# Small constants and statistics in pools of their own, and every large on-chip buffer at a multiple of 128 bytes

## The chip, the cores and the metric

The kernel runs on one core of one Trainium2 chip, as one program launched once. The metric is device time in microseconds (us) of one execution, the median of several. The engines named below are TensorE (PE, with its weight loads as PEld), VectorE (DVE), ScalarE (ACT), GpSimd (POOL) and SyncE (SP), whose queue issues the DMAs. The on-chip memory that all of them read is called SBUF here: 128 partitions, and in each partition the same byte addresses. A buffer's address is its byte address within a partition.

## The reference, cut to what matters

Two layers of a streaming encoder on 1024 tokens of width 1024, all in float32. Each layer normalises, projects, runs three families of attention heads, merges them, reads 256 memory tokens through a cross-attention, and ends with a squared-ReLU MLP of width 4096:

```python
for layer in range(2):
    h = rms_norm(x, mix_norm_g[layer])
    proj = h @ w_in[layer]
    da_q, da_k, da_v, sb_q, sb_k, sb_v, c_q, c_kv, k_r = jnp.split(proj, pts, axis=-1)
    y_a = diff_attention(...)      # 4 heads, two softmaxes each, T5 position bias
    y_b = stick_breaking(...)      # 4 heads, sigmoid gates and a reversed running product
    y_c = latent_attention(...)    # 4 heads through low-rank projections, with rope
    x = x + jnp.concatenate([y_a, y_b, y_c], axis=-1) @ w_out[layer]
    x = x + memory_attention(rms_norm(x, memx_norm_g[layer]), mem, ...)
    h = rms_norm(x, ffn_norm_g[layer])
    x = x + jnp.square(jax.nn.relu(h @ w_ff1[layer])) @ w_ff2[layer]
```

The first and third family are causal by chunks of 64 tokens, the second token by token.

## The kernel before

Tokens are cut in two halves of 512, and each half in tiles of 128. To keep float32 accuracy on TensorE's faster float32r form, every factor of a large product is split into a high and a low part, and `mm3` issues three matmuls for each product: high by high, high by low, low by high (lines 573, 574, 575). In a call `matmul(out, stationary, moving)` the first factor is loaded into the array and the second streams through it; the profile lists the moving operand first, so `s<-h,w 128x512` is a matmul whose moving operand is the 512 columns of a tile `h` and whose stationary one is a 128-column piece of `w`.

Weights arrive by DMA in 256 KB pieces as `raw`, and `wblock` splits each on ACT (line 551) and DVE (line 552) into `w`. Activations are normalised, transposed on TensorE against the identity (line 594), split, and held transposed in `h`. There is an `h` tile for each half: that of the first half lies in a pool that grows from the low end of SBUF ("left"), that of the second half in one that grows down from the top ("right"). The MLP computes 16 groups of 256 hidden columns: `ff1` streams `h` (512 columns) past pieces of `w` (lines 573 to 575), squares the result into `hid` or, in every second group of the last part, into two `t4` tiles, and `ff2` streams `w` (512 columns) past pieces of `hid` or `t4` (line 1266). `project` and `merge` mostly stream 256 columns of `w` past pieces of `h`. Attention runs once for each half (line 1007 scores, line 1042 weighted values).

Pools are laid out one after the other by the order in which they are opened. Each buffer in a pool is rounded up to 32 bytes. The left side begins at `_BASE`, 1152 bytes, which is 9 times 128; the right side ends at `_TOP`, 229344 bytes, which is 1791 times 128 and 96 more. The first pool, `const`, holds large pieces whose sizes are multiples of 128 bytes (among them `ident`, its first, at 1152 itself) and four small ones: `mhalf` (64 bytes), `zero1`, `neglam` and `gcol` (32 each with the rounding), 160 bytes together. So all pools behind `const` begin 32 bytes past a multiple of 128, and their large buffers lie there too: `w`, `raw`, `x`, `hid`, `r`, `t2`, `t4`, `cx` and the left `h`. The statistics (`ms`, `mt`, 64 bytes, six of each) lie in the pool `temps` between larger ones; they shift what is behind them by multiples of 64 bytes that add up to 128, so that some `t4` tiles stand 32 and some 160 past a multiple of 256. The right `h` and the buffers of the second half's attention lie 96 past a multiple of 128.

The order of the instructions is not that of the code. `order_engines` takes the whole program with ranks, simulates the engines with a table of costs, and fixes the order on every engine; what may go before what follows from the tiles' contents and from which pools overlap. The constants' preparation (`setup`, rank 8) is worked in beside the first projection. In `setup` two masks are loaded as `craw`, rounded on ACT to `crnd` and stored to a scratch in DRAM: one of 512 columns and one of 1024.

Of the kernel before, what the change touches and what calls it, by code (L numbers as in the profile page):

```python
# [9 lines left out]
F32 = mybir.dt.float32  # L10
F32R = mybir.dt.float32r
AF = mybir.ActivationFunctionType
# [5 lines left out]
P = 128  # L18
_BASE, _TOP = 1152, 229344
L = 2  # L20
S = 1024
# [321 lines left out]
def trunk(ctx: ExitStack, mem: Mem, tc: tile.TileContext, a: dict, out: bass.AP):  # L343
    nc = tc.nc
    HT = NT // 2
    HS = S // 2
# [8 lines left out]
    def f(ap):  # L355
        return ap.bitcast(F32)

    dma = nc.sync.dma_start
    cp = Pool("const")
    wp = Pool("wring")  # L360
    xyp = Pool("xy")
    hp = Pool("hid")
    tp = Pool("temps")
# [16 lines left out]
    def bank(cls):  # L380
        k = turn.get(cls, 0)
        turn[cls] = k + 1
        tag = cls[k % len(cls)]
        if tag[0] == "d":
            return more[1].tile([P, 1024], F32, tag=tag)[:, :512]
        return (psp if tag[0] == "s" else more[1]).tile([P, 512], F32, tag=tag)
# [10 lines left out]
    t4spare = [None]  # L397
# [13 lines left out]
        return tp.tile([P, 512], F32R, tag="cx", bufs=4)  # L411

    def stat():
        return tp.tile([P, 16], F32, tag="ms" if t4spare[0] is None else "mt", bufs=6)

    def newx(t):
        return f(xyp.tile([P, D], F32R, tag=f"x{t}"))
# [12 lines left out]
    def bcast_row(ap1d, n):  # L430
        return bass.AP(tensor=ap1d.tensor, offset=ap1d.offset, ap=[[0, P], [1, n]])

    def growload(src, n=D):
        g = cp.tile([P, D], F32, tag="grow", bufs=2)
        dma(g[:, :n], bcast_row(src[0:1], n))
        return g
# [9 lines left out]

    loadx(0, xin)
    gmix = growload(a["mix_norm_g"][0])
    mhalf = cp.tile([P, 16], F32, tag="mhalf")
    nc.vector.memset(mhalf, -0.5)  # L450
    zero1 = cp.tile([P, 1], F32, tag="zero1")
    nc.vector.memset(zero1, 0.0)
    flipR = cp.tile([P, P], F32R, tag="flip")
    before = cp.tile([P, 2, P], F32, tag="before")
    twin = cp.tile([P, 64], F32, tag="twin")
    cs = cp.tile([P, NT, 32], F32, tag="cs")
    neglam = cp.tile([P, L], F32, tag="neglam")
    lam_init = [0.8 - 0.6 * math.exp(-0.3 * l) for l in range(L)]
    gcol = cp.tile([P, L, 4], F32, tag="gcol")
    biasd = dp.tile([8, P, 2, 256], F32, tag="biasd")  # L460
    chunkd = [dp.tile([2 * HT, HS * (h + 1)], F32, tag=f"chunk{h}") for h in range(2)]

    def setup(pool):
        mraw = pool.tile([P, 2, P], F32, tag="mraw")
        dma(mraw, a["c_mask"][:2].rearrange("m p k -> p m k"))
        dma(before, a["c_mask"][2:].rearrange("m p k -> p m k"))
        dma(twin, a["c_twin"])
        nc.scalar.activation(flipR, mraw[:, 0, :], AF.Copy)

        for h in range(2):  # L470
            n = HS * (h + 1)
            craw = pool.tile([2 * HT, S], F32, tag="craw")
            dma(craw[:, :n], a[f"c_chunk{h}"])
            crnd = pool.tile([2 * HT, S], F32R, tag="crnd")
            nc.scalar.activation(crnd[:, :n], craw[:, :n], AF.Copy)
            dma(chunkd[h], f(crnd[:, :n]))

        lp = pool.tile([P, L, 4, 64], F32, tag="lp")
        dma(lp.rearrange("p l f d -> p (l f d)"), bcast_row(a["da_lambda"][0, 0, 0:1], L * 4 * 64))
        lprod = pool.tile([P, L, 2, 64], F32, tag="lprod")  # L480
        lpv = lp.rearrange("p l (u v) d -> p l u v d", v=2)
        nc.vector.tensor_tensor(lprod, lpv[:, :, :, 0, :], lpv[:, :, :, 1, :], op=ALU.mult)
        lsum = pool.tile([P, L * 2], F32, tag="lsum")
        nc.vector.tensor_reduce(lsum, lprod.rearrange("p l u d -> p (l u) d"), axis=AX.X, op=ALU.add)
        lexp = pool.tile([P, L * 2], F32, tag="lexp")
        nc.scalar.activation(lexp, lsum, AF.Exp)
        lev = lexp.rearrange("p (l u) -> p l u", u=2)
        nc.vector.tensor_tensor(neglam, lev[:, :, 1], lev[:, :, 0], op=ALU.subtract)
        for l in range(L):
            nc.vector.tensor_scalar(neglam[:, l:l + 1], neglam[:, l:l + 1], -lam_init[l], None, op0=ALU.add)  # L490

        oh = pool.tile([32, 384], F32, tag="oh")
        dma(oh, a["c_onehot"])
        rb = pool.tile([32, 2, 8], F32, tag="rb")
        dma(rb[:, 0, :], a["rel_bias"])
        far = a["rel_bias"][15, 0:1]
        dma(rb[:, 1, :], bass.AP(tensor=far.tensor, offset=far.offset, ap=[[0, 32], [1, 8]]))
        rd = pool.tile([32, 8], F32, tag="rd")
        nc.vector.tensor_tensor(rd, rb[:, 0, :], rb[:, 1, :], op=ALU.subtract)
        ps = bank(("e2",))  # L500
        nc.tensor.matmul(ps[:8, :384], rd, oh, start=True, stop=True)
        br = pool.tile([8, 384], F32, tag="br")
        nc.scalar.activation(br, ps[:8, :384], AF.Copy)
        bd = dp.tile([8, 384], F32, tag="bd")
        dma(bd, br)
        for m in range(8):
            tt = pool.tile([P, 256], F32, tag="bt", bufs=2)
            h0 = bd[m:m + 1, 0:1]
            dma(tt, bass.AP(tensor=h0.tensor, offset=h0.offset, ap=[[1, P], [1, 256]]))
            nc.vector.tensor_tensor(tt[:, 128:], tt[:, 128:], mraw[:, 1, :], op=ALU.add)  # L510
            bb = pool.tile([P, 2, 256], F32R, tag="bb", bufs=2)
            nc.scalar.activation(bb[:, 0, :], tt, AF.Copy)
            nc.vector.tensor_tensor(bb[:, 1, :], tt, f(bb[:, 0, :]), op=ALU.subtract)
            dma(biasd[m], f(bb))
# [62 lines left out]
    def rstd_of(ms, n, d):  # L577

        nc.vector.tensor_scalar(ms, ms, 1.0 / d, EPS, op0=ALU.mult, op1=ALU.add)  # L579
        rs = stat()[:, :n]  # L580
        nc.gpsimd.tensor_tensor(rs, ms, mhalf[:, :n], op=ALU.pow)  # L581
        return rs
# [20 lines left out]
    def norm_T(x_, grow, hi, lo, cls):  # L603

        xn = f(t4())
        ms = stat()
        nc.scalar.activation(xn, x_, AF.Square, accum_out=ms[:, 0:1])
        rs = rstd_of(ms[:, 0:1], 1, D)
        nc.vector.scalar_tensor_tensor(xn, x_, rs, grow, op0=ALU.mult, op1=ALU.mult)
        split_T(xn, hi, lo, cls)  # L610
# [23 lines left out]
    with ExitStack() as st:  # L634
        mem.rank(8, 20000.0)
        setup(Pool("setup", st=st))
        mem.rank(6, 8000.0)
        gains()
        mem.rank(0)
# [7 lines left out]
    for l in range(L):  # L647
# [29 lines left out]
        def project(h, pcls, cls, mid=None):  # L677
# [16 lines left out]
            def latent_in(t, cx, res):  # L694
                jk = f(t2())
                ms = stat()
                nc.scalar.activation(jk[:, :256], cx[:, :256], AF.Square, accum_out=ms[:, 0:1])
                nc.scalar.activation(jk[:, 256:384], cx[:, 256:384], AF.Square, accum_out=ms[:, 1:2])
                nc.vector.tensor_scalar(ms[:, 0:1], ms[:, 0:1], 0.5, None, op0=ALU.mult)
                rs = rstd_of(ms[:, 0:2], 2, 128)  # L700
                nc.vector.scalar_tensor_tensor(cx[:, :256], cx[:, :256], rs[:, 0:1], gcq, op0=ALU.mult, op1=ALU.mult)
                nc.vector.scalar_tensor_tensor(cx[:, 256:384], cx[:, 256:384], rs[:, 1:2], gckv,
                                               op0=ALU.mult, op1=ALU.mult)
                pt = bank(cls)[:, :384]
                transposes(pt, cx, 3)
                ct = t4()[:, :768].rearrange("p (s c) -> p s c", s=2)
                split(pt, ct[:, 0, :], ct[:, 1, :])
                res["ct"] = ct
# [727 lines left out]
```

## Time and profile before

| | |
|---|---|
| median of 3 runs | 2969.06 us (2963.79 to 2970.68) |
| the profiled execution's own time | 2966.24 us |
| its span from the first instruction to the last | 2964.5 us |
| matmuls, and TensorE busy | 16,818, 2880.0 us (97%) |
| VectorE busy | 1933.8 us (65%) |
| ScalarE busy | 1399.8 us (47%) |
| GpSimd busy | 464.1 us (16%) |
| share of the 16 DMA engines in use | 38.8% |

Matmuls are pipelined: the next one starts before the one ahead has ended, and the time given for one (some 390 ns for 512 columns) is longer than the distance to the next. How fast TensorE works is therefore read from the starts: the difference of two starts, divided by the number of matmuls between them, is the time that one costs. This is called the spacing below. 512 columns at one per cycle of 2.4 GHz take 213.3 ns, 256 take 106.7.

### The profile page before, as it was taken

The numbers are of one execution on the slowest core, as the hardware profiler recorded it, in microseconds if no ns is written. First come the engines' busy times: TensorE is split into PE (matmuls) and PEld (weight loads), VectorE is DVE, ScalarE is ACT, GpSimd is POOL, SyncE is SP. The second block draws the span as 40 slices with busy tenths as digits, with TensorE's granted clock in tenths as the row PEclk, the third lists the DMA queues.
The fourth block names the chain that finished last, engine by engine and source line by source line (L and its number), as shares of the span: only waits on it lengthen the run. The fifth ranks groups of instructions, "written<-read, shape, count | busy, mean of one in ns | idle before, by whom it ended". The sixth has DMA issues, their size and how long they took to land.

```text
span 2964.5 us, 46467 instructions
## 1 busy us (share of the span) xinstructions
PE 2880.0 (97%) x16818; PEld 2507.9 (85%) x16818; DVE 1933.8 (65%) x3715; ACT 1399.8 (47%) x3330; POOL 464.1 (16%) x556
## 2 busy tenths in 40 slices
PE   8989999899999999999999899998999999999999
PEld 7978999688898888888899789986888988888887
DVE  6878776887757544465567876768777574444555
ACT  5667555566644322133345674655666352122232
POOL 1452221421100000000013521324111000000000
PEclk9999999999999999999999999999999999999999
DMA  7766544534232111123257674444442322111232
GB/s 235 221 194 187 187 132 119 163 120 148 60 128 69 57 57 53 34 95 103 89 168 211 175 217 155 127 146 135 133 130 80 99 65 64 36 57 52 91 103 86
DMA packets 381205, 354.34 MB, mean 120 GB/s; under 512 B 27368, under 2 KB 301200, under 8 KB 380976
## 3 DMA queue, kind: packets, MB, share of 16 engines
q1 hardware_dynamic: 380976, 351.37, 38.8%
q8 instruction: 133, 2.18, 0.3%
q14 instruction: 96, 0.79, 0.1%
HBM read 290.40 MB, written 60.88 MB: 118 GB/s over the span
## 4 chain that ended last, share of the span: by engine, by line
PE 79%; DVE 7%; DMA 5%; issue 3%; ACT 3%; POOL 3%; SPq 1%; DVEq 0%; POOLq 0%; ACTq 0%
PE d L1266 17%; PE s L575 12%; PE s L574 12%; PE s L573 12%; PE s L1266 5%; PE s L594 4%; PE d L1007 3%; PE s L1027 2%; PE e L1007 2%; PE e L573 2%; PE e L575 2%; PE e L574 2%; DVE t L1121 1%; DMA raw<-in_w_in 1%; PE s L1042 1%
## 5 line engine op out<-in xcount | busy, mean ns | idle before, releaser
L551 ACT ACTIVATE w<-raw 128x512 fp32r<-128x512 f32 (+1 forms) x688 | 420.8, 626 | 553.1 <-PE d L1266 245.5
L552 DVE TENSOR_TENSOR w<-raw,w 128x512 fp32r<-128x512 f32 (+1 forms) x688 | 466.2, 690 | 195.5 <-ACT w L551 193.0
L573 PE MATMUL s<-h,w 128*128 128x512 f32 x1120 | 445.7, 398 | 1.2 <-ACT w L551 1.2
L575 PE MATMUL s<-h,w 128*128 128x512 f32 x1120 | 444.6, 397 | 0.0
L574 PE MATMUL s<-h,w 128*128 128x512 f32 x1120 | 443.7, 396 | 0.0
L1270 DVE TENSOR_TENSOR x<-d,x 128x1024 f32<-128x1024 f32 (+1 forms) x185 | 225.1, 1217 | 169.6 <-PE d L1266 169.6
L581 POOL TENSOR_TENSOR ms<-ms,mhalf 128x4 f32<-128x4 f32 (+3 forms) x144 | 148.0, 1030 | 1141.7 <-DVE ms L579 1138.1
L573 PE MATMUL s<-w,h 128*128 128x256 f32 (+1 forms) x1024 | 297.7, 295 | 4.9 <-ACT h L586 3.5
L575 PE MATMUL s<-w,h 128*128 128x256 f32 (+1 forms) x1024 | 298.4, 294 | 0.1
L574 PE MATMUL s<-w,h 128*128 128x256 f32 (+1 forms) x1024 | 297.4, 294 | 0.6 <-DVE w L552 0.6
L1266 PE MATMUL d<-w,hid 128*128 128x512 f32 x1152 | 267.0, 389 | 0.0
L1243 ACT ACTIVATE r<-s 128x512 f32<-128x512 f32 x128 | 76.6, 598 | 400.0 <-issue 232.8
L1245 DVE TENSOR_TENSOR r<-r 128x512 f32<-128x512 f32 x128 | 93.5, 730 | 258.5 <-ACT r L1243 258.3
L1266 PE MATMUL s<-w,hid 128*128 128x512 f32 x864 | 250.7, 411 | 10.6 <-ACT w L551 5.4
L1266 PEld LDWEIGHTS d<-w,hid 128*128 128x128 f32 x1152 | 216.2, 188 | 45.6
L1266 PE MATMUL d<-w,t 128*128 128x512 f32 x1056 | 248.5, 393 | 0.0
L575 PEld LDWEIGHTS s<-h,w 128*128 128x128 f32 x1120 | 210.5, 188 | 43.0 <-DVE w L552 0.6
L573 PEld LDWEIGHTS s<-h,w 128*128 128x128 f32 x1120 | 210.7, 188 | 42.3 <-ACT w L551 1.4
L574 PEld LDWEIGHTS s<-h,w 128*128 128x128 f32 x1120 | 210.6, 188 | 42.0
L1266 PEld LDWEIGHTS d<-w,t 128*128 128x128 f32 x1056 | 198.7, 188 | 44.9
L1063 POOL TENSOR_TENSOR sm<-sm,mhalf 128x1 f32<-128x1 f32 x192 | 128.9, 671 | 547.6 <-DVE sm L1062 426.8
L573 PEld LDWEIGHTS s<-w,h 128*128 128x128 f32 x1024 | 193.0, 190 | 7.0 <-ACT h L586 4.1
(337 smaller groups left out, 5997.3 us busy)
## 6 DMA issues: line engine op xcount, KB each, us to landing
raw<-in_w_ff SPq DMA_DIRECT2D x400, 256.0 KB
raw<-in_w_in SPq DMA_DIRECT2D x144, 256.0 KB
raw<-in_w_out SPq DMA_DIRECT2D x64, 256.0 KB
x<-in_x SPq DMA_DIRECT2D x16, 512.0 KB
o<-biasd SPq DMA_DIRECT2D x32, 256.0 KB
raw<-in_w_in SPq DMA_DIRECT2D x32, 208.0 KB
v<-sv SPq DMA_DIRECT2D x24, 256.0 KB
v<-mv SPq DMA_DIRECT2D x24, 256.0 KB
```

The lines of the kernel that those rows point to most:

```text
L551: nc.scalar.activation(w[:, 0, o], raw, AF.Copy)
L552: nc.vector.tensor_tensor(w[:, 1, o], raw, f(w[:, 0, o]), op=ALU.subtract)
L573: nc.tensor.matmul(ps, sh, mh, start=start, stop=False)
L574: nc.tensor.matmul(ps, sh, ml, start=False, stop=False)
L575: nc.tensor.matmul(ps, sl, mh, start=False, stop=stop)
L581: nc.gpsimd.tensor_tensor(rs, ms, mhalf[:, :n], op=ALU.pow)
L594: nc.tensor.transpose(ps[:, k * P:(k + 1) * P], src[:, k * P:(k + 1) * P], ident)
L1007: nc.tensor.matmul(ps[:, c:c + w], sta, mov, start=first, stop=last[c // 512] == i)
L1063: nc.gpsimd.tensor_tensor(sm, sm, mhalf[:, :1], op=ALU.pow)
L1245: nc.vector.tensor_tensor(r2, r, r, op=ALU.mult)
L1266: nc.tensor.matmul(parts[e], hd[i][:, s, tt], w[:, e * 512:(e + 1) * 512], start=first, stop=last)
L1270: nc.vector.tensor_tensor(xt[t][:, cols], ps, xt[t][:, cols], op=ALU.add)
```

## The change

Three things are done. The four small constants move from `const` to a pool `tiny` in front of it, where `mhalf` takes 160 bytes, so that the pool has 256. The statistics move from `temps` to a pool `stats` of their own. At the top end a pool `edge` of 96 bytes is opened first on the right, with one memset, so that the right side goes down from a multiple of 128. With that, all large buffers begin at a multiple of 128 bytes: by the sizes, all pools behind `tiny` and `stats` start 128 past a multiple of 256. In `setup`, the two masks are worked in pieces of 512 columns, one and two of them, in place of 512 and 1024.

```diff
+    edge = Pool("edge", side="right")
+    nc.vector.memset(edge.tile([P, _TOP % 128 // 4], F32, tag="edge"), 0.0)
+    tiny = Pool("tiny")
+    statp = Pool("stats")
     cp = Pool("const")
...
     def stat():
-        return tp.tile([P, 16], F32, tag="ms" if t4spare[0] is None else "mt", bufs=6)
+        return statp.tile([P, 16], F32, tag="ms" if t4spare[0] is None else "mt", bufs=6)
...
-    mhalf = cp.tile([P, 16], F32, tag="mhalf")
+    mhalf = tiny.tile([P, 40], F32, tag="mhalf")[:, :16]
...
-    zero1 = cp.tile([P, 1], F32, tag="zero1")
+    zero1 = tiny.tile([P, 1], F32, tag="zero1")
...
-    neglam = cp.tile([P, L], F32, tag="neglam")
+    neglam = tiny.tile([P, L], F32, tag="neglam")
...
-    gcol = cp.tile([P, L, 4], F32, tag="gcol")
+    gcol = tiny.tile([P, L, 4], F32, tag="gcol")
...
-            craw = pool.tile([2 * HT, S], F32, tag="craw")
-            dma(craw[:, :n], a[f"c_chunk{h}"])
-            crnd = pool.tile([2 * HT, S], F32R, tag="crnd")
-            nc.scalar.activation(crnd[:, :n], craw[:, :n], AF.Copy)
-            dma(chunkd[h], f(crnd[:, :n]))
+            for c in range(0, n, HS):
+                craw = pool.tile([2 * HT, HS], F32, tag="craw")
+                dma(craw, a[f"c_chunk{h}"][:, c:c + HS])
+                crnd = pool.tile([2 * HT, HS], F32R, tag="crnd")
+                nc.scalar.activation(crnd, craw, AF.Copy)
+                dma(chunkd[h][:, c:c + HS], f(crnd))
```

The instructions and their sizes stay as they are but for the memset and the masks (one more load, one more ACT copy, one more store). The fixed order changes only near the start: between the 117th and the 916th of the 16,337 matmuls that the program issues, and on the other engines in the same stretch; behind it all five engines have the same instructions in the same order. The lines of the changed kernel stand 5 or 6 further down.

On SP, the queue that issues the DMAs, around the mask pieces (`craw` loaded, `chunk` stored; `raw` are weight pieces, `rows` gains, `bd` and `bt` the position bias), it was:

```order
L548 DMA raw_554<-in_w_in 128x4x128
L476 DMA chunk_22_96<-crnd_114 8x512
L473 DMA craw_117<-in_c_chunk 8x1024
L476 DMA chunk_23_97<-crnd_119 8x1024
L548 DMA raw_558<-in_w_in 128x4x128
L442 DMA rows_411_2141<-in_da_subln_g 128x128
L548 DMA raw_628<-in_w_in 128x4x128
L442 DMA rows_411_2141<-in_sb_out_g 128x64
L548 DMA raw_632<-in_w_in 128x4x128
L442 DMA rows_411_2141<-in_mla_out_g 128x64
L505 DMA bd_144<-br_142 8x384
```

and it is:

```order
L554 DMA raw_570<-in_w_in 128x4x128
L482 DMA chunk_26_107<-crnd_125 8x512
L479 DMA craw_128<-in_c_chunk 8x512
L482 DMA chunk_27_108<-crnd_130 8x512
L479 DMA craw_133<-in_c_chunk 8x512
L554 DMA raw_574<-in_w_in 128x4x128
L554 DMA raw_644<-in_w_in 128x4x128
L447 DMA rows_417_2157<-in_da_subln_g 128x128
L447 DMA rows_417_2157<-in_sb_out_g 128x64
L554 DMA raw_648<-in_w_in 128x4x128
L447 DMA rows_417_2157<-in_mla_out_g 128x64
L482 DMA chunk_27_108<-crnd_135 8x512
```

The third piece's load stands ahead of one weight piece, and its store some rows later.

On PE a few rows further in time, at the transposes of the latent inputs (`cx`) and of one tile of `h` (from `t`), it was:

```order
L594 MATMUL s_144_546<-ident_78,cx_399 128x128 x3
L594 MATMUL e_167_675<-ident_78,cx_426 128x128 x3
L594 MATMUL s_120_367<-ident_78,t_116_353 128x128 x3
L573 MATMUL s_139_507<-h_289,w_498 128x512
L574 MATMUL s_139_507<-h_289,w_498 128x512
L594 MATMUL s_120_367<-ident_78,t_116_353 128x128
```

and it is:

```order
L600 MATMUL s_150_562<-ident_89,cx_415 128x128 x3
L600 MATMUL e_173_691<-ident_89,cx_442 128x128
L579 MATMUL s_145_523<-h_305,w_514 128x512
L580 MATMUL s_145_523<-h_305,w_514 128x512
L600 MATMUL e_173_691<-ident_89,cx_442 128x128 x2
L600 MATMUL s_126_383<-ident_89,t_122_369 128x128
```

Two 512-column matmuls go ahead of transposes that they stood behind; the other changes on PE are of this kind and length.

## Rows read from the trace of the kernel before

**Rows 1.** The page: busy time by engine, and the granted clock in 40 slices.
```profile
PE 2880.0 (97%) x16818; PEld 2507.9 (85%) x16818; DVE 1933.8 (65%) x3715; ACT 1399.8 (47%) x3330; POOL 464.1 (16%) x556
PEclk9999999999999999999999999999999999999999
```
**Rows 2.** The page: the chain that ended last, by engine.
```profile
PE 79%; DVE 7%; DMA 5%; issue 3%; ACT 3%; POOL 3%; SPq 1%; DVEq 0%; POOLq 0%; ACTq 0%
```
**Rows 3.** Busy time by stretch: length, then each engine's (instructions), clock, DMA share, GB/s.
```profile
0.00:300.00 300.00, 274.41 (x1780) 247.04 (x1780) 224.65 (x586) 189.90 (x528) 100.27 (x133) 0.98 0.69 210
300.00:500.00 200.00, 196.65 (x1592) 191.58 (x1591) 140.97 (x320) 114.75 (x296) 47.43 (x55) 1.00 0.47 142
500.00:620.00 120.00, 105.47 (x569) 84.76 (x568) 93.89 (x152) 71.15 (x156) 51.98 (x46) 0.97 0.50 148
620.00:950.00 330.00, 326.86 (x2089) 291.12 (x2087) 237.01 (x469) 185.53 (x448) 31.61 (x44) 1.00 0.35 106
950.00:1490.00 540.00, 540.00 (x2403) 441.89 (x2403) 283.73 (x365) 153.72 (x271) 3.29 (x6) 1.00 0.23 71
2440.00:2950.00 510.00, 510.00 (x2227) 416.39 (x2227) 255.01 (x318) 130.09 (x221) 0.55 (x1) 1.00 0.21 68
```
**Rows 4.** Timeline of PE, first layer's MLP, first half's h: start, length, line, tiles.
```profile
1104.10 0.39 PE L573 MATMUL s<-h,w 128*128 128x512 f32 x1
1104.32 0.39 PE L574 MATMUL s<-h,w 128*128 128x512 f32 x1
...
1109.54 0.39 PE L573 MATMUL s<-h,w 128*128 128x512 f32 x1
```
**Rows 5.** Timeline of PE, second layer's MLP, second half's h.
```profile
2839.51 0.39 PE L573 MATMUL s<-h,w 128*128 128x512 f32 x1
...
2841.85 0.39 PE L574 MATMUL s<-h,w 128*128 128x512 f32 x1
```
**Rows 6.** Timeline of PE, 256 columns: pieces of the first half's h, then the second's.
```profile
349.80 0.28 PE L573 MATMUL s<-w,h 128*128 128x256 f32 x1
...
351.00 0.28 PE L573 MATMUL s<-w,h 128*128 128x256 f32 x1
...
841.06 0.28 PE L574 MATMUL s<-w,h 128*128 128x256 f32 x1
...
841.89 0.28 PE L575 MATMUL s<-w,h 128*128 128x256 f32 x1
```
**Rows 7.** Timeline of PE, transposes in plain float32, moving operand ident.
```profile
410.05 1.04 PE L594 MATMUL e<-ident,x 128*128 128x128 f32 x8
410.92 0.38 PE L594 MATMUL e<-ident,t 128*128 128x128 f32 x2
```
**Rows 8.** Groups by shape, PE, 0 to 950 us: count, busy us, mean ns of one, idle before.
```profile
L573 PE MATMUL s<-w,h 128*128 128x256 f32 x464 | 130.9, 286 | 0.9 <-ACT w L551 0.9
L1266 PE MATMUL s<-w,hid 128*128 128x512 f32 x384 | 112.5, 411 | 5.4 <-ACT w L551 2.8 <-DVE sm L1062 1.3 <-DVE hid L1247 1.0
L573 PE MATMUL s<-h,w 128*128 128x512 f32 x181 | 73.6, 407 | 1.2 <-ACT w L551 1.2
L573 PE MATMUL e<-w,h 128*128 128x256 f32 x176 | 50.4, 287 | 0.0
L1042 PE MATMUL s<-t,v 128*128 128x256 f32 x208 | 37.1, 292 | 2.4 <-DVE t L587 1.3 <-DVE sm L1062 1.0
```
**Rows 9.** Waits of PE, whole span: line, releaser, us in total, times, longest.
```profile
PE s L1051 <- DVE u L1050: 13.8, 26, 1.2
PE s L594 <- DVE t L609: 7.9, 1, 7.9
```
**Rows 10.** The masks' load and rounding: duration ns least/median/most, first and last start.
```profile
L473 SPq DMA_DIRECT2D craw<-in_c_chunk x2: 289/330/370, 27.0 to 33.5; - x2
L475 ACT ACTIVATE crnd<-craw x2: 614/834/1055, 31.2 to 36.3; 8x512 fp32r<-8x512 f32 x1, 8x1024 fp32r<-8x1024 f32 x1
```
**Rows 11.** Busy time from 33 to 150 us, columns as in Rows 3.
```profile
33.00:150.00 117.00, 114.60 (x828) 108.25 (x828) 87.81 (x200) 69.49 (x155) 35.81 (x41) 1.00 0.76 234
```

## The prediction

> **What bounds the kernel now.** I read the busy times first: TensorE is busy for 97% of the span at the full granted clock, 2.4 GHz, and the next engine for 65% [rows 1]. The chain that ended last is 79% TensorE [rows 2]. By stretches there are two kinds. In the MLPs, from 950 to 1490 us and from 2440 to 2950 us, TensorE has no idle microsecond, while VectorE is busy for half the time and the DMA engines for less than a quarter. From 300 to 500 and from 620 to 950 us it is busy for 98 to 99%. Only from 0 to 300 and from 500 to 620 us does it idle, by 26 and 15 us [rows 3]; the second layer repeats the first. So the question is what sets the time of one matmul, and for that the starts have to be read.
>
> In the MLP of the first layer, with the first half's h, 24 matmuls of 512 columns start between 1104.10 and 1109.54 us: 226.7 ns each [rows 4]. With the second half's h, ten take 2.34 us: 234 ns each [rows 5]. Form, size, clock and free inputs are the same; the operands' addresses differ: h begins 32 bytes past a multiple of 128 in the one, 96 past in the other. With 256 columns the spacing is 120.0 ns where the stationary piece is of the first half's h, and 0.83 us over seven, 118.6 ns, where it is of the second half's [rows 6]. Streaming alone takes 213.3 and 106.7 ns. So every wide matmul pays 12 to 21 ns over its columns, and how much follows from where its operands lie. The 13.3 ns of rows 4 are just 32 columns, which is 128 bytes of a row: as if one more piece of 128 bytes were read for each pass.
>
> One operand already lies at a multiple of 128: ident, the moving operand of the transposes, at 1152. Eight of them take 0.87 us, 108.8 ns each [rows 7]. That is two cycles for each of 128 columns, 106.7 ns, and only about 2.1 ns more.
>
> **The change part by part.** (1) Alignment. It adds no instruction to the matmuls; it moves both operands of every large one to 128 past a multiple of 256. What that does to the spacing no row shows, so it is bounded from both sides. The best end is the 2.1 ns of rows 7: 215.4 ns for 512 columns, 108.8 for 256. The other end is the worst pattern of the trace, the 234 ns of rows 5, for all. Between them lies 226.7, if only the pairing of the two addresses matters. I take the best end, because the only row with an operand at such an address stands there, and because an excess of just 128 bytes has no reason left once rows begin on that boundary.
>
> The sum at that end, MLPs first: in the second layer 2227 matmuls take 510 us, 229.0 ns each; 13.6 ns less for each are 30 us. The first layer's stretch has 540 us, of which the same 5.9% are 32. TensorE alone paces both, and VectorE's 255 of 510 us leave room for a 6% faster pace [rows 3], so all 62 us reach the end.
>
> Outside, per layer up to 950 us: lines 573, 574 and 575 have 464 matmuls each of 256 columns on s and 176 each on e [rows 8], 1920 together; at 120.0 and 118.6 ns in about equal parts they save some 10.5 ns each, 20 us. The 208 of line 1042 save 2. Of 512 columns there are 384 on line 1266 and three times 181 [rows 8], 927 together, 13.6 ns each, 13 us. The groups left out (416 and 384 columns, scores) I estimate at a fifth more. That makes 42 us per layer. Of TensorE's 6030 instructions there, 3681 lie in the two full stretches [rows 3], 61%: 26 us, of which I let 80% through, since TensorE idles only 3 us in each now [rows 3]. Of the other 16 us, in stretches that end on chains through VectorE and ScalarE (line 1051 waits 26 times for line 1050 [rows 9]), I let 30% through. So 21 and 5, twice: 52 us.
>
> (2) The masks. One more load of about 0.33 us of SP's time, one more store of the like, and three ACT copies of 614 ns in place of one of 614 and one of 1055 [rows 10]: about 0.2 us more on ACT. The extra load stands ahead of one weight piece on SP and so delays it by a third of a microsecond. At that time TensorE is filled from 33 to 150 us for 114.6 of 117 us [rows 11], which hides it; uncovered it would be 1 us.
>
> (3) The changed order lies in the same stretch. It can win at most the 2.4 us that TensorE idles there [rows 11], and could lose as much as the longest single wait for VectorE in the trace, 7.9 us [rows 9]. I take nothing.
>
> (4) The memset of 24 columns is at the very start, while the first weights are on their way. Statistics and constants in other places keep the same instructions; they are on POOL and VectorE, and I take nothing, bounded by the same 2.4 us either way. Copies on VectorE and ScalarE and the DMAs get new addresses too; where TensorE paces, a gain there is hidden, and in the first 300 us, with 69% of the DMA engines' time in use [rows 3], it could add a few microseconds to the gain.
>
> Sum: 62 + 52 = 114 us off the profiled execution's 2966.2, which is 2852. The median of the runs stands 2.8 us higher: 2855.
>
> The Trainium skill, "TensorE: Matmul & The Clock Gate", section "Wait — 56ns, not 53.3ns?", gives back-to-back matmuls N divided by 2.4 GHz plus about 2.5 ns, 215.7 ns for 512 columns. The trace disagrees for these operands, by 11 to 18 ns [rows 4, 5]. By its figure for both widths the sum would be some 3 us smaller.
>
> **The rivals.** *Pairing only.* The excess of 13.3 ns belongs to the float32r form wherever it lies, and only unequal offsets of the two operands cost more. For it: w and the first half's h, both 32 past a multiple of 256, give the steadiest spacing of all [rows 4], and unequal ones the 234 ns [rows 5]. Against it: 120.0 ns with equal offsets is more than 118.6 with unequal ones [rows 6], and transposes pay almost nothing [rows 7]. Then the MLPs go from 229.0 to 226.7 ns, 1.0% of 1050 us or 10.5 us, and outside them the 512-column matmuls gain 2 us per layer and half of the 256-column ones lose 1.4 ns, 1.3 us: together 12 us off, 2957.
>
> *Nothing changes.* The addresses do not matter, and the two spacings have another cause, such as what else runs beside them. For it: VectorE, ScalarE and DMA traffic differ between the stretches. Against it: the spacing stays the same for 24 matmuls in a row, which traffic would not give. The time would be 2969. The Trainium skill, "SBUF — State Buffer", section "Specifications (TRN2)", has lines of 16 bytes, and by that rule a start at 32 bytes is as good as one at 128: it is this rival. Rows 4 and 5, both with starts at multiples of 32, speak against it by 7 ns.
>
> *A worse place.* At 128 past a multiple of 256, the two operands of every matmul meet as h and w of the second half do now, and the whole MLP goes at 234 ns. For it: no float32r row shows this offset, and unequal offsets show that some places are worse. Against it: ident lies at this offset. Price: 5 ns on 2227 matmuls and the like on the first layer's, 11 + 12 us, and 5 ns on 927 per layer outside, 9 us: 32 us more, 3001. It decides as soon as more than a third of the MLP's matmuls, which now run at 227 ns, go above 230.
>
> **How the numbers follow.** The best end has a chance of 0.64, pairing only 0.16, nothing 0.11, a worse place 0.09. About 0.2%, 6 us, is what a measurement of this kernel can tell from no change. Faster are the first case and most of the second: 0.77. The same are the third and the rest of the second: 0.14. Slower is the last: 0.09. The first case's own range goes from 2820, where all of the 42 us per layer comes through (62 + 84 off), to 2910, where the MLPs' gain alone does. To hold 8 in 10 the range must take in the second case and reach towards the third: 2820 to 2966.
>
> **What would show it.** Right: the spacing of 512 columns near 215.5 ns in both halves' MLP, that of 256 near 109, the MLP's stretches shorter by 30 us each with TensorE still without idle time, and TensorE's idle time in the attention stretches larger than before. If the spacing is 226.7 everywhere, it was pairing; if it is 227 and 234 as now, the addresses are not the cause; above 230 everywhere, a worse place. If the spacing falls and the time does not, the step on what comes through was wrong, and waits for VectorE (lines 552 and 1050) or for weights would have grown instead. The first 150 us would show the new order: more than 5 us of new idle time there would make parts 2 and 3 wrong.

## The result, and the profile after

The changed kernel takes 2951.30 us in the median of its runs (2949.77 to 2953.55), against 2969.32 for the kernel before: a ratio of 0.995, 95% interval 0.9938 to 0.9962, 18 us less. The forecast was 2855, 114 us less. Measured again later in another group of runs the ratio was 0.9962 (0.995 to 0.9973), 11 us less, so the gain is 11 to 18 us. Every group has the kernel before beside it, and ratios are to that one; a comparison across two groups is less sure by some microseconds.

The page of the changed kernel, in the order of [rows 1, 2]: busy time by engine, the granted clock, and the chain by engine.

```profile
PE 2865.3 (97%) x16818; PEld 2509.8 (85%) x16818; DVE 1931.2 (66%) x3716; ACT 1397.4 (47%) x3331; POOL 463.1 (16%) x556
PEclk9999999999999999999999999999999999999999
PE 81%; DVE 7%; DMA 4%; ACT 3%; POOL 2%; issue 2%; SPq 1%; DVEq 0%; POOLq 0%; ACTq 0%
```

TensorE's busy time is 14.7 us less with the same 16,818 matmuls, and the other engines are where they were. Busy time by stretch, columns as in [rows 3]; the last MLP's stretch ends earlier now:

```profile
0.00:300.00 300.00, 275.61 (x1807) 249.05 (x1808) 225.81 (x595) 191.76 (x538) 98.38 (x134) 0.98 0.70 213
300.00:500.00 200.00, 197.04 (x1578) 192.44 (x1577) 139.18 (x314) 112.86 (x287) 46.82 (x54) 0.99 0.46 138
500.00:620.00 120.00, 105.33 (x572) 84.00 (x571) 95.44 (x158) 71.50 (x159) 52.12 (x46) 0.99 0.51 149
620.00:950.00 330.00, 326.83 (x2084) 291.15 (x2083) 234.86 (x464) 185.05 (x443) 31.62 (x44) 1.00 0.34 106
950.00:1490.00 540.00, 540.00 (x2434) 448.56 (x2433) 287.91 (x370) 154.31 (x272) 3.29 (x6) 1.00 0.24 75
2430.00:2935.00 505.00, 505.00 (x2239) 418.45 (x2239) 255.53 (x319) 130.48 (x222) 0.55 (x1) 1.00 0.21 69
```

The stretches outside the MLPs hardly differ from [rows 3]: from 300 to 950 us the same idle time, 16 matmuls fewer of 4250. The MLPs got through more: in the first, 2434 matmuls in 540 us in place of 2403. The middle of the second MLP shows it best, since TensorE does little but 512-column matmuls there: 400 us from 2500 on, first of the kernel before, then of the changed one (length, TensorE's busy time and matmuls, clock, DMA share, GB/s):

```profile
2500.00:2900.00 400.00, 400.00 (x1740) 1.00 0.22 69
```
```profile
2500.00:2900.00 400.00, 400.00 (x1766) 1.00 0.23 72
```

That is 229.9 ns for each before and 226.5 now, 1.5%. Over the two MLP stretches of 1050 us it is 15 us, nearly the whole difference. The spacing itself, from PE's timeline in the MLPs of the first and second layer, then among matmuls of 256 columns and the transposes:

```profile
1104.30 0.39 PE L581 MATMUL s<-h,w 128*128 128x512 f32 x1
...
1109.74 0.39 PE L581 MATMUL s<-h,w 128*128 128x512 f32 x1
...
2829.62 0.39 PE L579 MATMUL s<-h,w 128*128 128x512 f32 x1
...
2833.70 0.39 PE L579 MATMUL s<-h,w 128*128 128x512 f32 x1
...
839.74 0.28 PE L581 MATMUL d<-w,h 128*128 128x256 f32 x1
...
841.06 0.28 PE L581 MATMUL s<-w,h 128*128 128x256 f32 x1
...
407.74 1.04 PE L600 MATMUL e<-ident,x 128*128 128x128 f32 x8
408.61 0.38 PE L600 MATMUL e<-ident,t 128*128 128x128 f32 x2
```

Between the first two lie 24 matmuls, 226.7 ns each, as in [rows 4]; between the next two 18, 226.7 too, where [rows 5] had 234. Eleven of 256 columns with the second half's h take 1.32 us, 120.0 ns each, where [rows 6] had 118.6: slower. The transposes are at 108.8 as in [rows 7]. In these rows nothing is below the better value of before: what was at 234 came to 227, and what was at 118.6 went up to 120.

Added up over all matmuls, the trace says where the 16.4 us between the two spans are. For each start I take how far it stands behind the streaming time of the matmul before it, one column per cycle of 2.4 GHz (two cycles for a transpose); up to 30 ns are counted as excess, and more as a gap. The excess of the 512-column matmuls fell from 114.0 to 98.5 us, that of the 256-column ones rose from 62.6 to 67.3, and the gaps fell from 283.9 to 278.3. The two kinds of excess together are 10.8 us less. The 5.6 us of the gaps prove nothing: in the later run of the same changed kernel they are 283.5. (The excess in an expectation below takes 2.5 ns more of each matmul as streaming, which changes such differences by some 0.2 us.) The largest waits of PE are the same two as in [rows 9] (waited for: us in total, times, longest):

```profile
PE s L1057 <- DVE u L1056: 12.7, 24, 1.2
PE s L600 <- DVE t L615: 8.0, 1, 8.0
```

### The profile page after: what moved, and what is told of

Same layout as the page of the kernel before. It is cut to its first block, busy times and chain, and to the rows that moved or that the text cites. A ratio compares the mean times of both kernels' runs of the same rounds, so it can differ in the third digit from the quotient of the medians.

```text
span 2948.1 us, 46476 instructions
## 1 busy us (share of the span) xinstructions
PE 2865.3 (97%) x16818; PEld 2509.8 (85%) x16818; DVE 1931.2 (66%) x3716; ACT 1397.4 (47%) x3331; POOL 463.1 (16%) x556
## 4 chain that ended last, share of the span: by engine, by line
PE 81%; DVE 7%; DMA 4%; ACT 3%; POOL 2%; issue 2%; SPq 1%; DVEq 0%; POOLq 0%; ACTq 0%
PE d L1272 17%; PE s L580 12%; PE s L581 12%; PE s L579 12%; PE s L1272 5%; PE s L600 4%; PE d L1013 3%; PE s L1033 2%; PE e L579 2%; PE e L581 2%; PE e L580 2%; PE e L1013 2%; DVE t L1127 1%; PE e L600 1%; PE s L1048 1%
```

## The experiments

**Matmuls alone.** TensorE alone runs series of 96 matmuls with the starts of both operands chosen; a to h stand for 0, 32, ... 224 bytes past a multiple of 256, the moving operand's letter first. It computes nothing of the reference.

```
series("big_aa", 512, 0, 0)        # float32r, 512 columns, both at 0
series("big_ba", 512, 8, 0)        # moving operand 32 bytes on
series("mid_ga", 256, 48, 0)       # 256 columns, moving operand 192 bytes on
series("bf_aa", 512, 0, 0, MB, WB) # the same in bfloat16
```

> A kernel of matmuls alone: 96 in a row of each kind, three high/low pairs in turn as in the real kernel, the moving operand starting at one offset past a multiple of 256 bytes (first letter: a 0, b 32, c 64, d 96, e 128, f 160, g 192, h 224) and the stationary at another (second letter); big is 512 columns, mid 256, few 128. It computes none of the reference. Pairing theory (the float32r form costs its columns plus 13.3 ns wherever it lies, and unequal offsets change that): big_aa, big_bb, big_cc, big_dd, big_ee all 226.7 ns, mid_aa, mid_bb, mid_dd, mid_ee all 120.0; big_ba to big_ha partly 231 to 234, mid shifted 113 to 120. Boundary theory (a start on a multiple of 128 saves a piece of 128 bytes, and something else holds the real kernel at 226.7): big_aa and big_ee near 215.5, big_bb, big_cc, big_dd 226.7. If the 13.3 ns come from the stationary operand's 128 columns of four bytes, half_aa and quarter_aa (64 and 32 stationary columns) and bf_aa (two bytes) are below it, bf_aa near 216; if from the moving side alone, half and quarter are 226.7 too.

PE's timeline of it: start of a series, its length, tile and operands.

```profile
60.86 21.93 PE L44 MATMUL big_aa<-M,W 128*128 128x512 f32 x96
82.63 21.96 PE L44 MATMUL big_bb<-M,W 128*128 128x512 f32 x96
...
148.01 21.95 PE L44 MATMUL big_ee<-M,W 128*128 128x512 f32 x96
169.80 22.57 PE L44 MATMUL big_ba<-M,W 128*128 128x512 f32 x96
192.21 22.14 PE L44 MATMUL big_ca<-M,W 128*128 128x512 f32 x96
214.18 22.57 PE L44 MATMUL big_da<-M,W 128*128 128x512 f32 x96
236.59 22.56 PE L44 MATMUL big_ea<-M,W 128*128 128x512 f32 x96
...
326.25 11.67 PE L44 MATMUL mid_aa<-M,W 128*128 128x256 f32 x96
...
372.28 11.37 PE L44 MATMUL mid_ba<-M,W 128*128 128x256 f32 x96
...
429.10 11.05 PE L44 MATMUL mid_ga<-M,W 128*128 128x256 f32 x96
439.99 11.52 PE L44 MATMUL mid_ha<-M,W 128*128 128x256 f32 x96
451.34 10.83 PE L44 MATMUL few_aa<-M,W 128*128 128x128 f32 x96
462.01 10.88 PE L44 MATMUL few_ea<-M,W 128*128 128x128 f32 x96
472.73 21.98 PE L44 MATMUL same_aa<-M,W 128*128 128x512 f32 x96
494.55 22.24 PE L44 MATMUL half_aa<-M,W 128*64 128x512 f32 x96
516.63 22.49 PE L44 MATMUL half_ga<-M,W 128*64 128x512 f32 x96
538.95 22.39 PE L44 MATMUL quarter_aa<-M,W 128*32 128x512 f32 x96
561.19 20.89 PE L44 MATMUL bf_aa<-MB,WB 128*128 128x512 bf16 x96
581.92 20.88 PE L44 MATMUL bf_ba<-MB,WB 128*128 128x512 bf16 x96
602.64 10.64 PE L44 MATMUL bfmid_aa<-MB,WB 128*128 128x256 bf16 x96
```

The mean distance from start to start within a series, its first twelve matmuls left out, is the spacing. Equal starts give 226.7 ns at 0, 32, 64, 96 and 128 alike, and so does one stationary piece throughout (same). Spacings by how far the moving operand stands past the stationary one, modulo 256 bytes; where the two differ, the stationary one was always at 0:

| bytes | 0 | 32 | 64 | 96 | 128 | 160 | 192 | 224 |
|---|---|---|---|---|---|---|---|---|
| 512 columns, ns | 226.7 | 233.4 | 228.9 | 233.4 | 233.4 | 234.3 | 233.4 | 233.4 |
| 256 columns, ns | 120.0 | 116.7 | 117.8 | 120.0 | 118.6 | 118.7 | 113.3 | 118.3 |

In bfloat16 512 columns take 215.8 ns at a distance of 0 and of 32 alike, and 256 columns 109.2 at 0. So the 13.3 ns over the streaming time, where bfloat16 has 2.5, go with the float32r form and come at every start tried, and in this run only the distance between the operands changes the spacing. The 13.3 ns do not shrink with the stationary piece: with 64 and 32 of its columns in place of 128 (half and quarter), at a distance of 0, the spacing is 230.0 and 231.7 ns.

Each matmul of the two programs priced by the distance of its operands, the stream of wide matmuls takes 2317.1 us in the kernel before (1654.0 and 663.1 for the two widths) and 2308.5 in the changed one (1637.5 and 671.0): 8.6 us less, where the excess in the traces fell by 10.8.

**The masks in pieces alone.** The kernel before with only the hunk on craw and crnd from the change.

> The kernel before with the masks in pieces of 512 alone, and with it nearly the changed order of the first 150 us; all addresses as before. Pairing theory and boundary theory: no change, within 3 us of 2969. Order theory (the gain comes from the first 150 us): 2951.

2967.97 us, ratio 0.9999 (0.999 to 1.0009). TensorE's order is that of the changed kernel, instruction for instruction, so the masks and the order they change are worth nothing that this measurement can tell (0.1% is 3 us).

**The right side alone.** The same and a right edge, so that h of the second half begins 32 past a multiple of 256, where w already lies:

```diff
+    edge = Pool("edge", side="right")
+    nc.vector.memset(edge.tile([P, 48], F32, tag="edge"), 0.0)
```

> As masks, with 192 bytes at the top of SBUF, so that the second half's h and its attention buffers lie 32 past a multiple of 256 like w, and no large buffer lies at a multiple of 128. Pairing theory: the spacing with the second half's h falls from 234 to 226.7 ns; some 1650 matmuls by 6 ns, 10 us less: about 2959. Boundary theory: no gain, 2969.

2961.75 us, ratio 0.9978 (0.9969 to 0.9987). No operand of a float32r matmul of 256 or more columns lies on a multiple of 128 in it, and 6 us of the gain are there. The expectation had counted the second half's 512 columns alone. Against the trace of the masks alone the excess of 512 columns is 10.6 us less, as it said, but that of 256 columns is 5.6 more.

**The statistics alone.** The masks again, and the statistics in a pool in front of the constants, which moves the rest of the left side to 32 past a multiple of 256:

```diff
+    statp = Pool("stats")
...
-        return tp.tile([P, 16], F32, tag="ms" if t4spare[0] is None else "mt", bufs=6)
+        return statp.tile([P, 16], F32, tag="ms" if t4spare[0] is None else "mt", bufs=6)
```

> The kernel before with its row masks written in pieces of 512, as in the change, and with the small statistics in a pool of their own in front of the constants, so that the big buffers of the left side all begin 32 bytes past a multiple of 256; the right side stays at 224. Offsets theory: only the distance between moving and stationary rows counts, and it is changed for the part of the left side that stood elsewhere; priced with the spacings of the run of matmuls alone, the stream of matmuls is 2.9 us shorter, so about 2965 us. Rival, the statistics in a pool of their own are what the change gains by (their slots are no longer among the temporaries, VectorE waits less): about 2957 us or less, near all of what is left when the 6.3 us of the run with the right side moved are taken from the 18 us.

2963.59 us, ratio 0.9989 (0.9979 to 0.9998): 2.4 us, about the 2.9 that the distances pay for. The pool by itself gains nothing that shows.

**Both, and the changed kernel again.** Edge, statistics and masks together in the kernel before; every large buffer is 32 past a multiple of 256.

> The kernel before with three parts at once: masks in pieces of 512, statistics in a pool in front of the constants, 192 bytes at the top of the right side. All large buffers then begin 32 bytes past a multiple of 256 on both sides, nothing on a multiple of 128. Offsets theory: as the changed kernel, 2949 to 2955 us. Sum of the parts as measured (6.3 us and 2.4 us): 2957 to 2960 us. Rival, the boundary of 128: no gain beyond the parts', 2960 us or more.

> The changed kernel itself, as the standard of this group. By its first runs 2951 us (ratio 0.9938 to 0.9962).

Both: 2958.18 us, ratio 0.9973 (0.9963 to 0.9982). The changed kernel: 2955.54, ratio 0.9962 (0.995 to 0.9973). The intervals overlap, and the excess of the two widths is the same in the traces, 165.2 and 165.8 us; the two parts, 6.3 and 2.4 us in their own groups, add up to the 8.1 of both. In the second MLP they go at one pace: the run of both starts 1766 matmuls in the 400 us from 2500 on, as the changed kernel does.

```profile
2500.00:2900.00 400.00, 400.00 (x1766) 1.00 0.23 72
```

The expected 2949 to 2955 was too low by 3 us, since I had set it by the changed kernel's first runs.

**32 past the boundary.** The changed kernel with everything 32 bytes further, on both sides:

```diff
-    nc.vector.memset(edge.tile([P, _TOP % 128 // 4], F32, tag="edge"), 0.0)
+    nc.vector.memset(edge.tile([P, 16], F32, tag="edge"), 0.0)
...
-    mhalf = tiny.tile([P, 40], F32, tag="mhalf")[:, :16]
+    mhalf = tiny.tile([P, 48], F32, tag="mhalf")[:, :16]
```

> The changed kernel, with all large buffers moved by 32 bytes to 160 past a multiple of 256, both sides alike: none begins at a multiple of 128, all have the same offset. Pairing theory: as the changed kernel, 2951 within 3 us, spacing 226.7 and 120. Boundary theory: 2969 or more.

2952.55 us, ratio 0.9947 (0.9935 to 0.996), as the change; the excess of the two widths is 166.0 us. With all large buffers off the boundary the gain is all there: the boundary plays no part.

**The weights 32 bytes further.** A test in the other direction: in the changed kernel, the main ring of weights is moved away from its partners.

```diff
+    Pool("low").tile([P, 8], F32, tag="low")
     wp = Pool("wring")
+    Pool("high").tile([P, 56], F32, tag="high")
```

> The changed kernel with the main ring of weights 32 bytes further, nothing else moved: 2400 matmuls of 512 columns then have their moving rows 32 past the stationary's and 2784 have them 224 past (226.67 to 233.35 ns each), and 2688 of 256 columns have 32 (120.0 to 116.65 ns). Offsets theory: 34.6 us more and 9.0 us less, a stream 25.6 us longer, so 2968 to 2977 us, slower than the changed kernel and no faster than the kernel before. Rival, the time of the change comes from the statistics and the masks and not from the spacing: within 3 us of 2951.

2980.09 us, ratio 1.0041 (1.0027 to 1.0054): by the ratios 23 to 27 us slower than the changed kernel, which was not run in this group, with one ring moved by 32 bytes and nothing else. The same 400 us of the second MLP hold 40 matmuls fewer:

```profile
2500.00:2900.00 400.00, 400.00 (x1726) 1.00 0.20 64
```

The prices gave 25.6 us; I had expected some of it to stay hidden (2968 to 2977 us), and little or none did. In the traces the excess of the two widths is 21.5 us larger.

**h 64 bytes further, everywhere and where it pays.** By the table, 256 columns want their moving operand 192 past the stationary one, and h is the stationary one there. In the first run every h moves by 64, between two small tiles; in the second only the h of the mixer and of the merge. The second's edit:

```diff
-    def newh(h):
-        return hpool[h].tile([P, 2, KT, HS], F32R, tag="h")
+    def newh(h, o=0):
+        t = hpool[h].tile([P, 2 * KT * HS + 64], F32R, tag="h")
+        return t[:, o:o + 2 * KT * HS].rearrange("p (s k c) -> p s k c", s=2, k=KT)
...
+        hnext[h] = newh(h, 16)
...
+            hY = newh(h, 16)
```

> The changed kernel with the MLP's hidden activations h 64 bytes further in their pools, nothing else moved. Offsets theory: 3456 matmuls of 512 columns that read h go from 226.67 to 228.85 ns, and 4224 of 256 columns whose stationary is h go from 120.0 to 113.33 ns (moving minus stationary is then 192 past a multiple of 256): 7.5 us more and 28.1 us less, a stream 20.6 us shorter; if between two thirds and all of it shows at the end, 2931 to 2938 us. Rival, begin at a multiple of 128 whatever the partner: 64 is off the boundary, so the time is 2951 us or more. Rival, spacing is hidden by other engines: within 3 us of 2951.

> The changed kernel with h 64 bytes further only where it is the stationary operand of the 256-column matmuls (the mixer's input and the merge's), and at the multiple of 128 where the MLP moves it. The run with h shifted everywhere measured, against the changed kernel, 8.9 us more over the 512-column matmuls, 16.0 us less over the 256-column ones and 9.5 us more of gaps over 30 ns, and the same time. Theory, the MLPs pay every spacing and the stages outside return about half: the 8.9 us go, the rest stays, so 2942 to 2946 us. Rival, outside the MLPs other engines set the pace and all is returned: 2950 to 2952 us. Rival, it is all paid by the spacings of the run of matmuls alone (28.1 us less, 0.8 us more): 2924 us.

Everywhere: 2951.55 us, ratio 0.994 (0.9924 to 0.9956), not clearly better than the change with its 0.995 and 0.9962; the forecast of 2931 to 2938 was wrong. The trace shows where it went. The 256-column excess fell by 16.1 us, not 28, the gaps grew by 9.4, and the 512-column excess grew by 9.1, where the table had 7.5: the middle of the second MLP holds 14 matmuls fewer than in the changed kernel.

```profile
2500.00:2900.00 400.00, 400.00 (x1752) 1.00 0.22 71
```

Where it pays: 2945.57 us, ratio 0.993 (0.9918 to 0.9942), the lowest time here. It is 10 us below the changed kernel of the same group (0.995 to 0.9973; the intervals do not meet). The MLP is back at its pace, and among matmuls of 256 columns with the first half's h nine now take 1.01 us, 112 ns each. With the second half's h, at the same distance of 192, eighteen take 2.12 us, 117.8 ns each:

```profile
2500.00:2900.00 400.00, 400.00 (x1767) 1.00 0.23 72
```
```profile
349.30 0.28 PE L580 MATMUL e<-w,h 128*128 128x256 f32 x1
...
350.31 0.28 PE L580 MATMUL e<-w,h 128*128 128x256 f32 x1
...
839.87 0.28 PE L581 MATMUL s<-w,h 128*128 128x256 f32 x1
...
841.99 0.28 PE L581 MATMUL s<-w,h 128*128 128x256 f32 x1
```

Over the 3807 matmuls of this kind that follow each other without a gap, the mean is 115.3 ns, most of them near 113 or near 118, against 119.6 in the changed kernel. So the table's 113.3 is reached only in part of the kernel, and the stream shortened by 16 to 17 us in place of 28. The two groups do not part by half alone (78 and 37% of the two halves are at 115 or below), and what parts them was not found.

Against the trace of the changed kernel of its group, its 256-column excess is 17.4 us less and its gaps are 10.0 more, and the span is 7.2 us shorter; the medians differ by 10. So outside the MLPs about half of a faster stream is given back as waiting.

**The 256-column weights 192 bytes further.** Another way to the same distance, in the rings of the weights; to make room, all small statistics share one set of six slots.

```diff
-        return statp.tile([P, 16], F32, tag="ms" if t4spare[0] is None else "mt", bufs=6)
+        return statp.tile([P, 16], F32, tag="ms", bufs=6)
...
-        w = wring[0]()
+        o = 48 if cw == 256 and wring[1] == 1024 else 0
+        w = wring[0]()[:, o:o + 2 * wring[1]].rearrange("p (s c) -> p s c", s=2)
```

> The changed kernel with the 256-column weights (the moving operand) 192 bytes further than everything else, in the ring of the last projection and in the ring of the merge, and all the rest at multiples of 256; the statistics share six slots, to make room. Offsets theory: 4608 matmuls of 256 columns go from 120.0 to 113.33 ns, 192 of 512 columns from 226.67 to 233.36: 30.7 us less and 1.3 us more, a stream 29.5 us shorter; with two thirds to all of it at the end, 2922 to 2932 us. Rival, multiples of 128 are what counts: 192 is not one, so 2951 us or more. Rival, hidden by other engines: within 3 us of 2951.

3069.65 us, ratio 1.0343 (1.0327 to 1.0358): far off. To tell its two edits apart, the shared slots ran alone, on the changed kernel.

> The changed kernel with one set of six slots for all small statistics instead of two sets (384 bytes left empty, so that every large buffer stays at a multiple of 128). In the run with the shifted 256-column weights this was one of two edits, and it stood still for about 50 us twice, near 440 to 600 and 1960 to 2100 us, with the clock at 0.6 to 0.8 there. Theory, the shared slots made that stall and the order around it: 3050 us or more here too. Rival, the shifted weights made it: 2948 to 2954 us.

3086.72 us, ratio 1.0407 (1.0392 to 1.0421): the shared slots did it. The kernel that shifts the weights too is some 17 us faster than this one, in another group of runs, so the shifted weights were no loss; in its trace the 256-column excess is 20 us less. The kernel with shared slots in two stretches, columns as in [rows 3]:

```profile
430.00:620.00 190.00, 153.56 (x863) 131.57 (x862) 100.99 (x180) 83.10 (x190) 40.87 (x39) 0.82 0.32 94
...
500.00:620.00 120.00, 92.10 (x401) 73.48 (x400) 60.59 (x96) 47.66 (x109) 24.19 (x23) 0.76 0.29 86
```

Its largest wait there (engine and line, waited for: us in total, times, longest):

```profile
POOL ms L588 <- DVE ms L586: 135.6, 20, 20.4
```

The changed kernel has 1125 matmuls from 430 to 620 us where this has 863, at a clock of 0.99, and its waits of POOL for the like are 54.5 us in all:

```profile
430.00:620.00 190.00, 175.33 (x1125) 151.80 (x1124) 142.76 (x257) 112.27 (x261) 64.39 (x59) 0.99 0.46 137
```
```profile
POOL ms L587 <- DVE ms L585: 37.4, 8, 12.8
POOL mt L587 <- DVE mt L585: 17.1, 4, 5.4
```

With shared slots every engine is less busy there, so none is at its limit: it is the order of the work and its waits that changed. The granted clock fell where TensorE paused, to 0.76 from 500 to 620 us, a mean of its two levels of 2.4 and 1.2 GHz, and adds to the loss. Which wait begins the stall, and how much is order and how much clock, was not told apart.

## Why the prediction was wrong

Part 1 failed at one sentence: "I take the best end, because the only row with an operand at such an address stands there, and because an excess of just 128 bytes has no reason left once rows begin on that boundary." The row was of transposes in plain float32, at 108.8 ns for 128 columns [rows 7]. It differs from the matmuls in form and in address, and I laid the whole difference to the address. The 13.3 ns go with the form: equal starts at 0, 32 and 128 past a multiple of 256 all show them, the same matmul in bfloat16 shows 2.5, and the kernel moved off the boundary is as fast as the one on it. That 13.3 ns equal 32 columns of 4 bytes proved nothing. Why float32r pays them stays open.

All of the 62 us in the MLPs and the 52 outside hung on that end. The measured time lies within the stated 2820 to 2966 us only because the range took in a rival; the sum is off by six to ten times. What came is the rival *pairing only*: 10.5 us forecast for the MLPs, about 15 measured; 512 columns at 226.7 in both halves, 256 columns at 120 in place of 118.6; 2957 forecast in all, 2951 measured, and 2955 in the second group. Its sign for the 256-column matmuls, which I had counted against it, was right: distance 0 is best for 512 columns and among the worst for 256. I gave it 0.16 although rows 4 and 5 already showed what it needs, one form and one size at two spacings where the operands' distance differs, and no row showed a float32r matmul without the excess.

What would have come through if the spacing had fallen was estimated at 80% in the full stretches and 30% in the others. For the MLPs "all of it" held, in both directions: the shifted weights' 25.6 us, most of them from 512-column matmuls, came as 23 to 27. Outside I had let through 26 of 42 us, 62%; the h shifted where it pays took 17.4 us out of the 256-column stream, and 7 of them by the two traces, 10 by the medians, came out at the end, 41 to 57%. That step was about right, on a stream that did not shorten as forecast.

Parts 2 and 3 were right as far as can be told: the masks and the new order change nothing (0.9999), though the stretch from 33 to 150 us [rows 11] did lose its idle time, 116.60 of 117 us busy now:

```profile
33.00:150.00 117.00, 116.60 (x851) 110.63 (x850) 87.20 (x202) 70.56 (x159) 33.61 (x41) 1.00 0.79 239
```

The 2 us won there would be too little to be seen at the end. Of part 4, the statistics in a pool of their own gain 2.4 us, and that by where they put their neighbours.

The other two rivals fell with the same runs. *Nothing changes*: 32 bytes of the weights' ring alone are 23 us or more. *A worse place*: 128 past a multiple of 256 is as good as any tried while both operands are there; it is the distance of 128 that costs 6.7 ns. The rule from the Trainium skill that stood beside the first of them ("SBUF — State Buffer", section "Specifications (TRN2)", lines of 16 bytes) does not tell operands at a distance of 0 from those at 32; the run of matmuls alone puts them 6.7 ns apart. The figure of the Trainium skill, "TensorE: Matmul & The Clock Gate", section "Wait — 56ns, not 53.3ns?", N divided by 2.4 GHz plus about 2.5 ns, is met in bfloat16 (215.8 and 109.2 ns) and missed in float32r by 11 ns.

Not settled: the changed kernel gained 18 us in its first group and 11 in the second, where the distances pay for 8.6 by the prices and 10.8 by the traces. The granted clock goes with most of the spread between the groups: its mean over the runs of the changed kernel was 0.9952 in the first and 0.9940 in the second. A straight line through all runs of these kernels but the two with shared slots (an estimate) puts 0.001 of clock at some 2.1 us. At one clock the changed kernel is then 13 to 15 us below the kernel before in both groups, the kernel 32 past the boundary 14, and the run of both parts 10; the kernel with the weights moved is 25 us above the changed one. The few microseconds between the changed kernel and the run of both parts lie in the gaps, since the excess of both is the same; whether anything else in the change gives them can't be told at this size.

## What to carry to other kernels

Before an excess in a matmul's spacing is laid to its address, compare rows of the same number form, or run the matmul by itself at a few starts: one run of 618 us settled what the sum of 114 us hung on. In float32r, place buffers by the distance between the two operands and by the width, equal starts for 512 columns and another distance for 256, role by role, and read the spacing again in the kernel itself: 113.3 ns alone became 115.3 on average there. Take a microsecond saved in the stream of matmuls as a microsecond only where TensorE has no idle time, and as about half elsewhere, as far as these runs show.

## What the runs showed of the hardware

- In the run of matmuls alone the spacing of float32r matmuls depends on the distance of moving and stationary rows modulo 256 bytes: 226.7 to 234.3 ns for 512 columns, 113.3 to 120.0 for 256. At a distance of 0 it does not matter which of the starts tried both have. For 256 columns the best distance of those tried is 192, and 0 and 96 are the worst; in the kernel a distance of 192 gave 115.3 ns on average, near 113 in places and near 118 in others.
- With 64 or 32 stationary columns in place of 128, 512 columns of float32r at a distance of 0 start 230.0 and 231.7 ns apart, not sooner.
- Bfloat16 shows nothing of it at the one other distance tried: 215.8 ns for 512 columns at 0 and at 32.
- Matmuls of 128 columns in float32r, each with a stationary operand of its own, start 111 to 112 ns apart, not half of the 120 ns of 256 columns; at a distance of 128 it is the same.
- Six slots for small statistics in place of twice six cost 131 us (3086.72 against 2955.54 in one group), with a granted clock of 0.76 in the stretch where TensorE paused.
